# The first up product of an MLP from operands without the norm's factor, and half of a branch product's rows, in a form with seven products

## The chip, the cores and the metric

One NeuronCore of one Trainium2 chip runs the whole program. The metric is device time in microseconds. A time of a kernel is the median of several executions; one further execution is taken by the hardware profiler, and all views of the profile come from that one. TensorE is called PE, VectorE DVE, ScalarE ACT, GpSimd POOL and SyncE SP, as in the profile.

## What is computed

One decoder layer for 512 prompt tokens and 8 x 4 sample tokens, all in float32. Cut to what the change touches:

```python
    # y_a: retention branch, 2048 wide; y_b: gMLP branch, 1024 wide
    merged = sigmoid(zga) * (y_a @ w_br_a) + sigmoid(zgb) * (y_b @ w_br_b)
    h = h + merged @ w_o
    n2 = rmsnorm(h, g_mlp)
    h = h + square(relu(n2 @ w_up)) @ w_down        # w_up: 1024 x 4096, w_down: 4096 x 1024
```

`rmsnorm` multiplies each token by `rsqrt(mean(h*h) + eps)` and each feature by `g_mlp`. The factor of a token is positive, so `relu` may be taken before or after it.

## The kernel before

**Layout.** All activations are kept transposed: a tile holds 128 features on the partitions and all T = 544 tokens in its columns. A product runs over tokens in two halves of TH = 272 columns, so one output tile of 128 features takes two PSUM banks (`Product`, line 303). D = 1024 makes KD = 8 tiles. The MLP's 4096 middle features are worked in four parts f = 0 to 3 of 1024 each: an up product, then a down product that is added to the residual tiles `hs`.

**Precision.** Each float32 operand is split in a high part, rounded to the `float32r` format by ACT, and a low part, the rest, which DVE subtracts (`split`, lines 130 and 131). Each product is then three matmuls: high x high, high x low, low x high.

**The plain form.** `tile_of` (line 327) takes one weight slab (128 x 1024: eight k tiles of one output tile) and issues 8 x 3 x 2 = 48 matmuls of 128 x 272 through `dense` (line 310). `first_two` (line 469) works the first two tiles of a product side by side over the first six k tiles and only then over the last two, so that the last operands of the product may come late. `tiles_from` (line 477) yields all eight tiles.

**The form with seven products.** `fast_run` (line 393) makes two output tiles at once over eight k tiles. Weights, operands and result are looked at as 2 x 2 blocks: the two output tiles by the two halves of the k tiles, those by the two halves of the tokens. Sums and differences of blocks let seven block products stand for eight. A block product is 4 k tiles x 3 matmuls. The operand blocks are B00, B10, B11 and the sums T1 to T4, which `operand_steps` (line 339) makes from a pair of operand tiles k and k + 4: four additions of 272 columns (lines 346 to 355), and the splits of the blocks and of the sums. An operand whose split parts exist already can be handed in as `plain`. The weight blocks of a pair of slabs need a sum that a DMA makes (POOL's queue adds the second slab to two loaded halves, line 207), two additions of 512 columns on DVE (lines 254 and 255) and splits of three slabs and a half, where two plain slabs need two. The block products are drained one by one: copies by ACT (lines 429, 443), and sums on DVE (lines 437 to 459). With two tiles as its target a run adds to these, with a function it returns new tiles with the function applied. A run that is listed in `late` takes three of the four k steps of its first three block products (T1, B10 and B00) before it needs the fourth pair of operands.

**Staging.** Around the change the order of the program is: the sigmoids of the gates (`sig_a`, `sig_b`); the second branch's product (8 plain tiles, line 1188) times `sig_b`; the first branch's product (lines 1193 to 1202: 8 tiles of 16 k tiles each, two weight slabs a tile, all in one PSUM accumulation), times `sig_a`, plus the other branch, split: `merged`; w_o (line 1208), added to the input x, which SP loads again: `hs`. Of each `hs` tile the up operand is made by `scaled_split` (line 525: ACT rounds x times `g_mlp`, DVE makes the rest), without the token's factor, and its square is summed (`add_square`). The first up product (line 1252) is plain. After its first tile `norm2` (line 1219) sums the squares over the features with four small matmuls (line 518) and makes the factor `r2` (root, then reciprocal, line 522). Each up tile is multiplied by it, squared and split (`up`, line 1223): `mid`. `normed_operands` (line 1239) makes, from `hs` and now with the factor in it, the operand sets for the later up products f = 1 to 3, which all run in the form with seven products; two sets are made in the up stage, two in the first down product (line 1258), which is plain. Then come the other parts (line 1298).

The first branch's operands `ya` are 16 tiles of 128 features, stored in DRAM by the heads; `head_tile` (line 1179) loads and splits them while the second branch's product runs, at half-steps given in `HEADS`.

**What sets the order.** `chores` and `later` hang a piece of work on a coming half-step: `tick` runs at every second k tile of `dense` and at every block product of `fast_run`, and calls what is due. `Feed` plans the weights in the order of their use, loads them ahead on SP's queue (five slab buffers, sums looked for two jobs ahead) and splits up to six parts ahead. The program so written is then put in order by a planner, which places each engine's instructions by when it reckons their inputs to be ready, earlier ones in the program first; so neighbouring products can be interleaved on PE. `pin` keeps an instruction behind all that stand before it in the program on its engine. Temporary tiles come from 70 numbered slots (`Slots`, line 65), reused oldest first.

Of the kernel before, what the change touches and what calls it, by code (L numbers as in the profile page):

```python
# [9 lines left out]
F32R = mybir.dt.float32r  # L10
# [4 lines left out]
P = 128  # L15
# [13 lines left out]
GROUPS = 8  # L29
SLAB = 1024  # L30
# [25 lines left out]
HEADS = (0, 2, 4, 6, 8, 10, 12, 14, 16, 18, 20, 21, 22, 23, 24, 25)  # L56
# [37 lines left out]
def layer(tc, a, o):  # L94
    nc = tc.nc
    act, dve, pool, pe = nc.scalar, nc.vector, nc.gpsimd, nc.tensor
    with ExitStack() as ctx:
# [379 lines left out]
        def tiles_from(xs):  # L477

            yield from first_two(xs, (range(KD - 2), range(KD - 2, KD)))
            for _ in range(2, KD):  # L480
                yield tile_of(xs)
# [64 lines left out]
        for m in range(KD):  # L546
            for i in range(2):
                feed.plan("plain", a["w_br_a"][8 * i + m])
        for k in range(8):
            feed.plan("plain", a["w_o"][k])  # L550
        for n in ("w_up", "w_down"):
            for k in range(8):
                feed.plan("plain", a[n][k])
# [8 lines left out]

        plan_up(1, range(4))
# [613 lines left out]
        ya = [None] * 4 * H  # L1177
# [8 lines left out]

        chores([(n, head_tile, k) for k, n in enumerate(HEADS)])
# [4 lines left out]
        merged = []  # L1192
        for m in range(KD):
            ps, t = Product(), get()
            for i in range(2):
                w = feed.take()
                xw = [(*at(w, k * P), *ya[8 * i + k]) for k in range(KD)]
                dense(ps, xw, first=i == 0, last=i == 1)
            dve.tensor_tensor(out=halves(t), in0=ps.all, in1=halves(sig_a[m]), op=ALU.mult)
            dve.tensor_tensor(out=t, in0=t, in1=sig_b[m], op=ALU.add)  # L1200
            put(sig_a[m], sig_b[m])
            merged.append(operand(t))
        for x in ya:
            put(*x)

        hs, hg = [None] * KD, [None] * KD
        total = get()
        for m, ps in enumerate(tiles_from(merged)):
            x = hs[m] = get()
            nc.sync.dma_start(x, a["xT"][m * P : (m + 1) * P, :])  # L1210
            dve.tensor_tensor(out=halves(x), in0=halves(x), in1=ps.all, op=ALU.add)
            hg[m] = scaled_split(x, g(G_MLP, m))
            add_square(total, x, m == 0)
        for x in merged:
            put(*x)
# [7 lines left out]
        def up(ps, k):  # L1223
            t = get()
            if k < 2:
                act.activation(halves(t), ps.all, AF.Relu)
                if k == 0:
                    norm2()
                dve.tensor_tensor(out=t, in0=t, in1=r2s["r"], op=ALU.mult)
            else:  # L1230
                dve.scalar_tensor_tensor(
                    out=halves(t), in0=ps.all, scalar=0.0, in1=halves(r2s["r"]), op0=ALU.max, op1=ALU.mult
                )
            act.activation(t, t, AF.Square)
            return operand(t)

        normed = []

        def normed_operands(k):
            x2 = get(), get()  # L1240
            for i in range(2):
                m = k + 4 * i
                dve.scalar_tensor_tensor(
                    out=x2[i], in0=hs[m], scalar=g(G_MLP, m), in1=r2s["r"], op0=ALU.mult, op1=ALU.mult
                )
# [5 lines left out]
        mid = []  # L1251
        for k, ps in enumerate(tiles_from(hg)):
            mid.append(up(ps, k))
            if k in (3, 5):
                normed_operands(k // 2 - 1)
        for x in hg:
            put(*x)
        for m, ps in enumerate(tiles_from(mid)):
            if m < 2:
                normed_operands(m + 2)  # L1260
            dve.tensor_tensor(out=halves(hs[m]), in0=halves(hs[m]), in1=ps.all, op=ALU.add)
# [293 lines left out]
```

## Time and profile before

| | |
|---|---|
| median of 3 runs | 1239.39 us (1238.52 to 1240.31) |
| the profiled execution | 1238.44 us, of which 1236.8 us are the span of the profile |
| granted TensorE clock | 0.996 |
| second branch's product, first branch's, w_o | about 615.7 to 663.9, to 760.4, to 808.7 us |
| first up product, first down product | to 857.5, to 906.0 us |
| second up product (seven products) | to 948 us |

The profile is of one execution; times in it are microseconds from the start of the span. "L131" is line 131 of the kernel. A group `out<-in` names the program's tiles: `s` a slot, `hl` a split weight slab, `raw` a loaded one, `f` a pair of PSUM banks, `fa` a single bank of `fast_run`. PEld is the weight load that each matmul has, beside the matmuls. A busy time or a mean of one instruction counts each instruction from its start to its end; where instructions of an engine overlap, the distance from start to start is shorter.

### The profile page before, as it was taken

To read this page: it belongs to the slowest core of one execution; us is meant where nothing else is said; L and a number is where in the kernel's file an instruction comes from. 1 tells how busy PE (TensorE), PEld (TensorE's weight loads), DVE (VectorE), ACT (ScalarE), POOL (GpSimd) and SP (SyncE) were. 2 spreads that over 40 slices of the span, in tenths; PEclk is the share of its full clock that TensorE was granted. 3 is DMA by queue.
4 is the path that set the end of the run, shared out by engine and by line. 5 is a ranking of instruction groups with operands and counts; after the bars stand their busy time and mean duration, and the time that the engine had idled before them with its cause. 6 is when DMAs were issued, how large, how long until landed. Compare 5 with 4: busy or idle time off the path is not lost.

```text
span 1236.8 us, 23016 instructions
## 1 busy us (share of the span) xinstructions
PE 1220.6 (99%) x9336; PEld 1192.5 (96%) x9336; DVE 895.9 (72%) x1333; ACT 636.6 (51%) x1082; POOL 92.4 (7%) x127
## 2 busy tenths in 40 slices
PE   9999999999999999999999999999999999999996
PEld 9998998998999999999999999999999999999996
DVE  6986888786697669878663333559459888878956
ACT  6563465365356366655641222455248567476733
POOL 0101101101111112100000000000000000000000
PEclk9999999999999999999999999999999999999998
DMA  8348546636735576665642333324446666764402
GB/s 282 129 156 268 188 136 240 208 131 208 240 115 178 162 220 177 182 160 162 217 156 88 115 107 105 103 69 120 103 111 173 186 180 154 193 183 127 139 1 73
DMA packets 73241, 193.15 MB, mean 156 GB/s; under 512 B 8400, under 2 KB 11728, under 8 KB 73136
## 3 DMA queue, kind: packets, MB, share of 16 engines
q1 hardware_dynamic: 59760, 143.65, 35.1%
q0 software_dynamic: 13376, 48.04, 16.3%
q8 instruction: 73, 1.20, 0.4%
q14 instruction: 32, 0.26, 0.1%
HBM read 165.97 MB, written 25.69 MB: 155 GB/s over the span
## 4 chain that ended last, share of the span: by engine, by line
PE 92%; DVE 4%; ACT 2%; DMA 1%; issue 1%; SPq 0%; DVEq 0%; ACTq 0%
PE f L318 41%; PE fa L407 20%; PE f L407 15%; PE o L494 2%; PE pg L318 2%; PE st L494 2%; PE sc L494 1%; PE su L892 1%; PE so L889 1%; PE so L890 1%; DVE s L522 1%; DVE hl L131 1%; ACT hl L130 1%; PE sp L1124 1%; PE vt L835 1%
## 5 line engine op out<-in xcount | busy, mean ns | idle before, releaser
L318 PE MATMUL f<-s,hl 128*128 128x272 f32 x4320 | 567.2, 289 | 1.2 <-ACT s L528 1.0
L318 PEld LDWEIGHTS f<-s,hl 128*128 128x128 f32 x4320 | 555.1, 188 | 8.2 <-ACT s L528 1.2
L130 ACT CAST hl<-raw 128x1024 fp32r<-128x1024 f32 (+2 forms) x275 | 262.1, 961 | 265.8 <-PE f L318 147.6
L131 DVE TENSOR_TENSOR hl<-raw,hl 128x1024 fp32r<-128x1024 f32 (+2 forms) x275 | 303.3, 1111 | 109.3 <-ACT hl L130 108.9
L407 PE MATMUL fa<-s,hl 128*128 128x272 f32 x2112 | 291.7, 289 | 1.1 <-ACT s L429 0.5
L407 PEld LDWEIGHTS fa<-s,hl 128*128 128x128 f32 x2112 | 274.0, 188 | 2.6 <-ACT s L429 0.7
L407 PE MATMUL f<-s,hl 128*128 128x272 f32 x1584 | 225.0, 289 | 0.7 <-DVE hl L131 0.5
L407 PEld LDWEIGHTS f<-s,hl 128*128 128x128 f32 x1584 | 208.3, 188 | 1.8 <-DVE hl L131 0.8
L130 ACT CAST s<-s 128x544 fp32r<-128x544 f32 (+3 forms) x170 | 97.9, 596 | 28.0 <-DMA s<-ya 6.5
L131 DVE TENSOR_TENSOR s<-s,s 128x544 fp32r<-128x544 f32 (+3 forms) x170 | 107.2, 657 | 4.2 <-ACT s L130 2.8
L893 DVE SCALAR_TENSOR_TENSOR state<-state,su 128x512 f32<-128x512 f32 x64 | 42.9, 681 | 27.3 <-PE su L892 27.2
L130 ACT CAST s<-state 128x512 fp32r<-128x512 f32 x64 | 37.9, 619 | 24.0 <-DMA state<-in_state 8.9
L131 DVE TENSOR_TENSOR s<-state,s 128x512 fp32r<-128x512 f32 x64 | 42.4, 684 | 7.7 <-ACT s L130 4.4
L522 DVE RECIPROCAL s<-s 128x544 f32<-128x544 f32 (+1 forms) x9 | 28.6, 3173 | 18.4 <-ACT s L520 18.4
L207 POOL DMA_DIRECT2D raw<-in_w_up x12 | 10.2, 850 | 412.9 <-DVE s L131 300.0
L454 DVE TENSOR_TENSOR s<-s,f 128x544 f32<-128x544 f32 x44 | 31.4, 713 | 9.4 <-PE f L407 9.1
L644 ACT COPY s<-f 128x544 f32<-128x544 f32 x24 | 14.7, 611 | 38.7 <-PE f L318 38.7
L443 ACT COPY s<-fa 128x272 f32<-128x272 f32 x44 | 16.9, 385 | 32.7 <-PE fa L407 32.5
L255 DVE TENSOR_TENSOR raw<-raw 128x512 f32<-128x512 f32 x44 | 30.4, 694 | 0.6
L254 DVE TENSOR_TENSOR raw<-raw 128x512 f32<-128x512 f32 x44 | 30.5, 695 | 0.4
L318 PE MATMUL pg<-s,s 128*128 128x272 f32 x240 | 30.8, 289 | 0.0
L318 PEld LDWEIGHTS pg<-s,s 128*128 128x128 f32 x240 | 30.3, 188 | 0.1
(175 smaller groups left out, 1103.8 us busy)
## 6 DMA issues: line engine op xcount, KB each, us to landing
raw<-in_w_in SPq DMA_DIRECT2D x58, 512.0 KB, 3.7
state<-in_state SPq DMA_DIRECT2D x32, 512.0 KB, 4.6
out_state_s<-state POOLq DMA_DIRECT2D x32, 512.0 KB, 4.1
raw<-in_w_in SPq DMA_DIRECT2D x60, 256.0 KB, 4.3
raw<-in_w_in POOLq DMA_DIRECT2D x20, 512.0 KB, 5.8
raw<-in_w_up SPq DMA_DIRECT2D x20, 512.0 KB, 3.8
raw<-in_w_down SPq DMA_DIRECT2D x20, 512.0 KB, 4.2
raw<-in_w_up SPq DMA_DIRECT2D x36, 256.0 KB, 3.3
```

What stands on the lines that cost most here:

```text
L130: act.copy(hi, src)
L131: dve.tensor_tensor(out=lo, in0=src, in1=hi.bitcast(F32), op=ALU.subtract)
L254: dve.tensor_tensor(out=t[:, 512:], in0=t[:, 512:], in1=v[:, :512], op=ALU.add)
L255: dve.tensor_tensor(out=t[:, :512], in0=t[:, 512:], in1=v[:, 512:], op=ALU.add)
L318: pe.matmul(ps.p[s], w, x[:, s * TH : (s + 1) * TH], start=first and i == 0 and j == 0, stop=last and i == n - 1 and j == 2, skip_group_ch ...
L407: pe.matmul(ps, a_, b_, start=first and k == j == 0, stop=k == 3 and j == 2, skip_group_check=True)
L443: act.copy(t0[:, hi_half], pa)
L454: dve.tensor_tensor(out=halves(x0), in0=halves(x0), in1=out.all, op=ALU.add)
L494: pe.matmul(ps[:rows, c], u, v, start=i == 0 and j == 0, stop=i == n - 1 and j == 2)
L522: dve.reciprocal(r[:, c], r[:, c])
L644: act.copy(halves(t), ps.all)
L893: dve.scalar_tensor_tensor(out=raw[:, i], in0=raw[:, i], scalar=gamma**LS, in1=ps, op0=ALU.mult, op1=ALU.add)
```

## The change

The first branch's product is cut in its k tiles. The first eight (heads 0 and 1) stay plain: `tiles_from(ya)`, each result copied to a slot by ACT (`sums`). The second eight (heads 2 and 3) go through `fast_run` and are added to these. `head_pair` loads their tiles in pairs and makes the operand sets in steps. The merge with the gates is then done by two DVE operations and a split from the slots, as chores of the next group.

The first up product goes through `fast_run` too, with operands that have `g_mlp` but not the token's factor in them. So w_o's tiles are made in the order 0, 4, 1, 5, 2, 6, 3, 7 (`PAIRED`); of each, ACT makes the scaled tile, which is split, and after the second of a pair the sums are made and split. The factor is applied after `relu`. The operand sets with the factor are now all made in the first down product, which takes its k tiles and its output tiles in the paired order. The first up product's weights are planned as four pairs, the first branch's second half as four pairs.

```diff
+PAIRED = (0, 4, 1, 5, 2, 6, 3, 7)
-HEADS = (0, 2, 4, 6, 8, 10, 12, 14, 16, 18, 20, 21, 22, 23, 24, 25)
+HEADS = (2, 4, 6, 8, 10, 12, 14, 16)
+PAIRS = (2, 8, 14, 20)
+UP = (0, 1)
+NORMED = (5, 10, 18, 25)
...
         for m in range(KD):
-            for i in range(2):
-                feed.plan("plain", a["w_br_a"][8 * i + m])
-        for k in range(8):
+            feed.plan("plain", a["w_br_a"][m])
+        for m in range(8, 16, 2):
+            feed.plan("fast", a["w_br_a"][m], a["w_br_a"][m + 1])
+        for k in PAIRED:
             feed.plan("plain", a["w_o"][k])
...
+        plan_up(0, range(4))
+        for k in PAIRED:
+            feed.plan("plain", a["w_down"][k])
...
+        def head_pair(k):
+            t2 = get(), get()
+            for i in range(2):
+                nc.sync.dma_start(t2[i], ya_d[KD + k + 4 * i])
+            res, held, steps = operand_steps(*t2)
+            y_ops.append((res, held))
+            steps[2:3] = [lambda fn=steps[2]: (fn(), put(*t2))]
+            for n, fn in enumerate(steps):
+                later(3 + n, fn)
...
-        merged = []
-        for m in range(KD):
-            ps, t = Product(), get()
-            for i in range(2):
-                w = feed.take()
-                xw = [(*at(w, k * P), *ya[8 * i + k]) for k in range(KD)]
-                dense(ps, xw, first=i == 0, last=i == 1)
-            dve.tensor_tensor(out=halves(t), in0=ps.all, in1=halves(sig_a[m]), op=ALU.mult)
+        chores([(n, head_pair, k) for k, n in enumerate(PAIRS)])
+        sums = []
+        for ps in tiles_from(ya):
+            sums.append(get())
+            act.copy(halves(sums[-1]), ps.all)
+        for x in ya:
+            put(*x)
+        merged = [None] * KD
+
+        def merge(m, t):
+            dve.tensor_tensor(out=t, in0=t, in1=sig_a[m], op=ALU.mult)
             dve.tensor_tensor(out=t, in0=t, in1=sig_b[m], op=ALU.add)
             put(sig_a[m], sig_b[m])
-            merged.append(operand(t))
+            merged[m] = operand(t)
+
+        for i, t2 in enumerate(fast_run([(y_ops, (sums[2 * i], sums[2 * i + 1])) for i in range(4)], (0,))):
+            if i < 3:
+                chores([(j, merge, 2 * i + j, t) for j, t in enumerate(t2)])
+            else:
+                for j, t in enumerate(t2):
+                    merge(2 * i + j, t)
...
-        for m, ps in enumerate(tiles_from(merged)):
+        for m, ps in zip(PAIRED, tiles_from(merged)):
             x = hs[m] = get()
             nc.sync.dma_start(x, a["xT"][m * P : (m + 1) * P, :])
             dve.tensor_tensor(out=halves(x), in0=halves(x), in1=ps.all, op=ALU.add)
-            hg[m] = scaled_split(x, g(G_MLP, m))
+            t = scaled[m] = get()
+            act.activation(t, x, AF.Copy, scale=g(G_MLP, m))
+            hg[m] = get(F32R), get(F32R)
+            split(*hg[m], t)
             add_square(total, x, m == 0)
+            if m >= 4:
+                x2 = scaled[m - 4], t
+                hg_ops.append(operands(*x2, (hg[m - 4], hg[m])))
+                put(*x2)
...
-                dve.scalar_tensor_tensor(
+                pin(dve.scalar_tensor_tensor(
                     out=x2[i], in0=hs[m], scalar=g(G_MLP, m), in1=r2s["r"], op0=ALU.mult, op1=ALU.mult
-                )
+                ))
...
-        mid = []
-        for k, ps in enumerate(tiles_from(hg)):
-            mid.append(up(ps, k))
-            if k in (3, 5):
-                normed_operands(k // 2 - 1)
+        mid = [None] * KD
+
+        def up(m, t):
+            dve.tensor_tensor(out=t, in0=t, in1=r2s["r"], op=ALU.mult)
+            act.activation(t, t, AF.Square)
+            mid[m] = operand(t)
+
+        for k, t2 in enumerate(fast_run([(hg_ops, AF.Relu)] * 4, (0,))):
+            if k == 0:
+                norm2()
+            for i, t in enumerate(t2):
+                later(UP[i], lambda m=k + 4 * i, t=t: up(m, t))
+        chores([(n, normed_operands, k) for k, n in enumerate(NORMED)])
...
-        for m, ps in enumerate(tiles_from(mid)):
-            if m < 2:
-                normed_operands(m + 2)
+        for m, ps in zip(PAIRED, tiles_from(mid, PAIRED[:6], PAIRED[6:])):
             dve.tensor_tensor(out=halves(hs[m]), in0=halves(hs[m]), in1=ps.all, op=ALU.add)
```

More of the change, by code (lines that the diff above doesn't have):

```diff
@@ L475, in first_two, with tiles_from @@
             return ps
-        def tiles_from(xs):
-            yield from first_two(xs, (range(KD - 2), range(KD - 2, KD)))
+        def tiles_from(xs, *turns):
+            yield from first_two(xs, turns or (range(KD - 2), range(KD - 2, KD)))
             for _ in range(2, KD):
@@ L546, in layer @@
         for m in range(KD):
-            for i in range(2):
-                feed.plan("plain", a["w_br_a"][8 * i + m])
-        for k in range(8):
+            feed.plan("plain", a["w_br_a"][m])
+        for m in range(8, 16, 2):
+            feed.plan("fast", a["w_br_a"][m], a["w_br_a"][m + 1])
+        for k in PAIRED:
             feed.plan("plain", a["w_o"][k])
-        for n in ("w_up", "w_down"):
-            for k in range(8):
-                feed.plan("plain", a[n][k])
         def plan_up(f, ks):
@@ L1176, in layer @@
             put(*held)
-        ya = [None] * 4 * H
+        ya, y_ops = [None] * KD, []
         def head_tile(k):
@@ L1191, in layer @@
             put(*x)
-        merged = []
-        for m in range(KD):
-            ps, t = Product(), get()
-            for i in range(2):
-                w = feed.take()
-                xw = [(*at(w, k * P), *ya[8 * i + k]) for k in range(KD)]
-                dense(ps, xw, first=i == 0, last=i == 1)
-            dve.tensor_tensor(out=halves(t), in0=ps.all, in1=halves(sig_a[m]), op=ALU.mult)
+        chores([(n, head_pair, k) for k, n in enumerate(PAIRS)])
[8 more added lines that the diff above has]
+            dve.tensor_tensor(out=t, in0=t, in1=sig_a[m], op=ALU.mult)
             dve.tensor_tensor(out=t, in0=t, in1=sig_b[m], op=ALU.add)
             put(sig_a[m], sig_b[m])
-            merged.append(operand(t))
-        for x in ya:
-            put(*x)
-        hs, hg = [None] * KD, [None] * KD
+            merged[m] = operand(t)
[5 more added lines that the diff above has]
+                    merge(2 * i + j, t)
+        for _, held in y_ops:
+            put(*held)
+        hs, hg, scaled, hg_ops = [None] * KD, [None] * KD, [None] * KD, []
         total = get()
-        for m, ps in enumerate(tiles_from(merged)):
+        for m, ps in zip(PAIRED, tiles_from(merged)):
             x = hs[m] = get()
@@ L1221, in norm2 @@
             put(total)
[L1223 to L1230, printed above, removed]
-                dve.scalar_tensor_tensor(
-                    out=halves(t), in0=ps.all, scalar=0.0, in1=halves(r2s["r"]), op0=ALU.max, op1=ALU.mult
-                )
-            act.activation(t, t, AF.Square)
-            return operand(t)
         normed = []
@@ L1242, in normed_operands @@
                 m = k + 4 * i
-                dve.scalar_tensor_tensor(
+                pin(dve.scalar_tensor_tensor(
                     out=x2[i], in0=hs[m], scalar=g(G_MLP, m), in1=r2s["r"], op0=ALU.mult, op1=ALU.mult
-                )
+                ))
             normed.append(operands(*x2))
@@ L1249, in normed_operands @@
                 put(r2s["r"])
-        mid = []
-        for k, ps in enumerate(tiles_from(hg)):
-            mid.append(up(ps, k))
-            if k in (3, 5):
-                normed_operands(k // 2 - 1)
+        mid = [None] * KD
[9 more added lines that the diff above has]
+        chores([(n, normed_operands, k) for k, n in enumerate(NORMED)])
         for x in hg:
             put(*x)
-        for m, ps in enumerate(tiles_from(mid)):
-            if m < 2:
-                normed_operands(m + 2)
+        for _, held in hg_ops:
+            put(*held)
+        for m, ps in zip(PAIRED, tiles_from(mid, PAIRED[:6], PAIRED[6:])):
             dve.tensor_tensor(out=halves(hs[m]), in0=halves(hs[m]), in1=ps.all, op=ALU.add)
```

## The prediction

> **What bounds the kernel now.** I read the page first: the engines' shares, then the chain that ended last.
>
> ```profile
> span 1236.8 us, 23016 instructions
> ...
> PE 1220.6 (99%) x9336; PEld 1192.5 (96%) x9336; DVE 895.9 (72%) x1333; ACT 636.6 (51%) x1082; POOL 92.4 (7%) x127
> ...
> PE 92%; DVE 4%; ACT 2%; DMA 1%; issue 1%; SPq 0%; DVEq 0%; ACTq 0%
> ```
>
> PE carries 92% of the chain and is busy for 99% of the span. That is an average, so I then took busy times in the stages that the change touches. I found their limits by counting 48 matmuls a plain tile back and forth from the norm's four small matmuls, which are easy to find. The columns are window, length, PE, PEld, DVE, ACT, POOL, granted clock, DMA share, GB/s.
>
> ```profile
> 663.90:712.00 48.10, 48.10 (x385) 48.10 (x384) 16.51 (x18) 10.35 (x11) 0.00 (x0) 1.00 0.31 100
> 712.00:760.40 48.40, 48.40 (x388) 48.40 (x386) 17.78 (x20) 10.98 (x12) 0.00 (x0) 1.00 0.35 117
> 760.40:808.70 48.30, 48.30 (x387) 48.30 (x386) 25.35 (x31) 17.32 (x23) 0.00 (x0) 1.00 0.30 94
> 808.70:857.50 48.80, 48.80 (x388) 48.64 (x388) 38.42 (x55) 26.58 (x40) 0.84 (x1) 1.00 0.30 86
> 857.50:906.00 48.50, 48.50 (x389) 48.50 (x387) 23.16 (x31) 12.37 (x15) 2.55 (x3) 1.00 0.45 110
> 906.00:948.00 42.00, 42.00 (x337) 42.00 (x336) 33.96 (x53) 31.26 (x54) 2.58 (x3) 1.00 0.56 147
> 948.00:958.50 10.50, 10.50 (x86) 10.50 (x85) 10.32 (x18) 8.52 (x17) 0.87 (x1) 1.00 0.60 145
> ```
>
> The rows are the first branch's product (two), w_o, the first up product, the first down product, the second up product (already in the form with seven products), and one more group of that form. PE's busy time equals the window in every one, at clock 1.00: nothing can be won here but by fewer matmuls, and every microsecond that PE waits afterwards is lost. DVE has much spare time in the first rows (16.5 of 48.1) and none in the last (10.32 of 10.50), and yet PE loses nothing there.
>
> What a matmul costs shows in PE's timeline, from start to start:
>
> ```profile
> 821.52 84.64 PE L318 MATMUL f<-s,hl 128*128 128x272 f32 x672
> 906.00 1.67 PE L407 MATMUL fa<-s,hl 128*128 128x272 f32 x12
> 907.51 1.66 PE L407 MATMUL f<-s,hl 128*128 128x272 f32 x12
> 909.00 3.17 PE L407 MATMUL fa<-s,hl 128*128 128x272 f32 x24
> ```
>
> The plain form: 84.48 us for 672, so 125.7 ns. The other form: 3.00 us for 24, so 125.0 ns. One price serves both, and I take 125.6 ns. The two stages meet at 906.00 without a gap, a plain stage followed by one of seven products, which is what the change makes twice more. The mean durations on the page (289 ns) overlap and are no price.
>
> **What is removed.** Two output tiles over eight k tiles take 2 x 8 x 3 x 2 = 96 matmuls in the plain form, and 7 x 4 x 3 = 84 in the other. The up product has four such pairs and half of the first branch's rows four: 8 x 12 = 96 matmuls, 96 x 125.6 ns = **12.06 us**. The Trainium skill, "TensorE: Matmul & The Clock Gate", section "Back-to-back issue gap", gives N/2.4 + 2.5 ns for an isolated warm matmul, 115.8 ns at 272 columns, by which the gain would be an estimated 11.1 us; the trace's 125.6 differs and decides.
>
> **What is added, and whether it hides.** All of it lies on DVE, ACT and the DMA queues. I price DVE from a stretch in which it runs without a break, again from start to start:
>
> ```profile
> 989.11 0.43 DVE L450 TENSOR_TENSOR s<-s,fa 128x272 f32<-128x272 f32 x1
> 989.47 1.23 DVE L131 TENSOR_TENSOR hl<-raw,hl 128x1024 fp32r<-128x1024 f32 x1
> 990.62 0.71 DVE L454 TENSOR_TENSOR s<-s,f 128x544 f32<-128x544 f32 x1
> 991.25 1.22 DVE L131 TENSOR_TENSOR hl<-raw,hl 128x1024 fp32r<-128x1024 f32 x1
> 992.38 0.44 DVE L131 TENSOR_TENSOR s<-s,s 128x272 fp32r<-128x272 f32 x1
> 992.73 0.43 DVE L437 TENSOR_TENSOR s<-s,f 128x272 f32<-128x272 f32 x1
> 993.08 0.69 DVE L254 TENSOR_TENSOR raw<-raw 128x512 f32<-128x512 f32 x1
> 993.68 0.43 DVE L459 TENSOR_TENSOR s<-s,fa 128x272 f32<-128x272 f32 x1
> 994.06 0.69 DVE L131 TENSOR_TENSOR hl<-raw,hl 128x512 fp32r<-128x512 f32 x1
> 994.67 0.69 DVE L255 TENSOR_TENSOR raw<-raw 128x512 f32<-128x512 f32 x1
> 995.27 0.72 DVE L131 TENSOR_TENSOR s<-s,s 128x544 fp32r<-128x544 f32 x1
> 995.90 0.72 DVE L445 TENSOR_TENSOR s<-s,s 128x544 f32<-128x544 f32 x1
> ```
>
> So 1.14 us for 1024 columns, 0.63 for 544, 0.60 for 512, 0.35 for 272. The weights of a pair cost 3 x 1.14 + 3 x 0.60 = 5.2 us of DVE where two plain slabs cost 2.3; a group of seven products gives PE 84 x 0.1256 = 10.55 us of work.
>
> First branch, second half. Per group: weights 5.2, the sums taken out of PSUM 3 x 0.35 + 2 x 0.63 = 2.3, and two merges of three 544-column operations each, 3.8. The first group has no merge yet (7.5); the next two need 11.3; the last splits plain w_o slabs instead (4.6 + 2.3 + 3.8 = 10.7). DVE falls behind by 0.75 + 0.75 + 0.15 = 1.7 us. After PE's last product there remain these 1.7, one PSUM sum 0.35, two merges 3.8 and the hand-offs to ACT and back, about 1: 6.9 us. w_o's first two tiles run six of eight k tiles first, 72 matmuls = 9.0 us, before they need the last merged tile. So it hides with 2 us to spare, and I take 0.3; if that cover is gone because a group's merges slip behind whole, it is 6.9 + 3.8 - 9.0 = 1.7. Below nothing is excluded: PE waits for nothing there today. The first half's evacuations (0.65 on ACT for each tile) and the operands from the stored heads (four times 4 x 0.35 + 0.35 + 3 x 0.63 = 3.6 us on DVE) fall into a stage with 30 us free: 0, with 0.2 for the entry, at most 1. The heads' loads move from one per tile of the second branch's product to pairs in the stage after it; on SP's queue they stand among weight loads with a 0.31 DMA share: 0.
>
> w_o into up. Here the cover shrinks. Before, the last w_o tile's operand was hidden by 9.0 us of matmuls. Now up's first group runs three of four k steps of its first three products and one more: 27 + 3 = 30 matmuls, 3.77 us, and then wants a sum of the last tile. How such an end of a w_o tile runs, on DVE and on ACT:
>
> ```profile
> 808.98 0.72 DVE L1211 TENSOR_TENSOR s<-s,f 128x544 f32<-128x544 f32 x1 [2.35 <-PE f L318]
> 810.11 1.23 DVE L131 TENSOR_TENSOR hl<-raw,hl 128x1024 fp32r<-128x1024 f32 x1 [0.41 <-ACT hl L130]
> 811.25 0.78 DVE L529 SCALAR_TENSOR_TENSOR s<-s,gcols,s 128x544 fp32r<-128x544 f32 x1
> 811.95 0.72 DVE L504 TENSOR_TENSOR s<-s,s 128x544 f32<-128x544 f32 x1
> ```
>
> ```profile
> 809.03 1.05 ACT L130 CAST hl<-raw 128x1024 fp32r<-128x1024 f32 x1 [3.79 <-issue]
> 809.98 0.75 ACT L528 ACTIVATE s<-s,gcols 128x544 fp32r<-128x544 f32 x1
> 810.63 0.64 ACT L503 ACTIVATE s<-s 128x544 f32<-128x544 f32 x1
> ```
>
> PE ends at about 808.9. A weight slab's cast goes first on ACT (its buffer came free), so the scaled tile, now an ACT step of its own, is there at 0.1 + 0.95 + 0.65 = 1.7 us, its rounded part at 2.35, the square at 3.0. DVE meanwhile: slab 2.2, rest of the tile 2.95, square's sum 3.6, first two sums 4.3; ACT rounds them by 4.95; DVE does the next two sums to 5.0 and the rest of the first two to 5.6. So 5.6 us against 3.77. PE's queue can hold other ready work there: three k steps of the fourth product (9), the last step of another (3), the next group's first product (12), 24 matmuls or 3.0 us, and the planner does put such work forward (the 24 `fa` matmuls at 909.00 are two products of one bank name side by side, out of program order). This is the one wait that the change adds: PE's fourth k step of the second product waits for DVE, and behind it in the queue stands all of up that was not put forward. The cost is between 0 and 1.9, up to 3.0 if a second cast slips in; I take 1.0.
>
> Up into down. The norm's factor is applied after the seven products: per group weights 5.2, sums 0.35 + 0.63, factor and rest for two tiles 4 x 0.63, in all 8.7 of 10.55. The reciprocal was there before. The four operand sets for the next up products leave this stage for the down stage (each 2 x 0.69 + 4 x 0.35 + 0.35 + 3 x 0.63 = 5.0 us, on a DVE that is at 23.16 of 48.50 with two of them in it). They are now pinned to program order on DVE, so they can't be drawn ahead of the last pair's factor; behind them wait only the down product's sums, whose readers come a product later: 0. The last pair's chain of about 5.4 us (relu, factor, square, split, twice overlapped) has 9.0 us of matmuls as cover: 0, at most 1. The last operand set is called 7 of 32 half-steps before the end, 10 us ahead, and needs 5: 0, and 5 if that cover were gone.
>
> The sum: -12.06 + 0.2 + 0.3 + 1.0 = **-10.6**. The profiled execution took 1238.44 us (span 1236.8 and 1.64 around it), which makes 1227.9; the median of the three runs, 1239.39, stands 0.95 above that execution, so the forecast for a median is **1228.8**.
>
> **The rivals.** (1) *DVE sets the pace of the new stages and the covers fail.* 1.7 at w_o, 3.0 at up, 1 at the entry, 1 at down: 6.7 of the 12.06 is given back, 1239.39 - 5.4 = 1234.0. For it: the merges make 11.3 us of DVE in 10.55. Against: the 948.00 window, and three windows in a row within the up stage, of which these are the first and the last, cost PE nothing with DVE full.
>
> ```profile
> 827.00:837.50 10.50, 10.50 (x86) 10.50 (x85) 10.47 (x16) 7.22 (x12) 0.00 (x0) 1.00 0.17 54
> ...
> 848.00:858.50 10.50, 10.50 (x86) 10.50 (x85) 10.50 (x18) 5.35 (x9) 0.84 (x1) 1.00 0.64 137
> ```
>
> There, though, much of DVE's work was not yet wanted by anyone (operand sets for the next product), as the merges are wanted only at w_o.
>
> (2) *The weight sums come late, and the kernel gets slower.* Each pair needs two half loads, then an accumulating DMA on POOL's queue:
>
> ```profile
> L207 POOL DMA_DIRECT2D raw<-in_w_up x12: 842/848/855, 851.3 to 1078.1; - x12
> ...
> DMA to landing us min/median/max: 5.2/5.6/8.6
> ...
> raw<-in_w_up SPq DMA_DIRECT2D x36, 256.0 KB, 3.3
> ```
>
> That is 3.3 + 0.85 + 5.6 = 9.7 us one after the other, within a group's 10.55; at the longest landing 12.7, over by 2.2. If each of the eight new groups paid 2.2, the gain becomes 17.6 - 12.06 = 5.5 us of loss, 1244.9; the point of decision is 12.06 / 8 = 1.5 us a group. SP's queue is where it would show first, a load waiting for a buffer ahead of others. Against: windows 906 and 948 have the same traffic and lose nothing, and the loader in the code looks two jobs ahead for sums to load. The Trainium skill, "SBUF — State Buffer", section "SBUF: two separate sides", says that descriptors for DMAs from GpSimd cannot be written while some DVE operations hold the shared port, so a busier DVE would delay just these transfers. By that rule this rival is the likelier the fuller DVE is; the trace's issue times of 842 to 855 ns, in stretches with DVE nearly full, do not bear it out.
>
> (3) *Nothing measurable*: the same lateness near 1.5 us a group.
>
> **How the numbers follow.** Forecast 0.77, first rival 0.15, third 0.04, second 0.04. About 0.2% (2.5 us) is what a measurement of this kernel can tell from no change. Faster: 0.77 + 0.15 = 0.92; same 0.04; slower 0.04. The low end is the whole 12.06 less 0.9 for the scatter of the runs (1238.52 to 1240.31), 1226.4; the high end takes in the first rival and a microsecond of scatter, 1235.0.
>
> **What would show it.** Right: 96 matmuls fewer, still some 125.6 ns apart; PE busy 12 us shorter; DVE busier by some 60 us (weights 8 x 2.9, the operand sums and PSUM sums the rest); no PE gap over 0.5 us but one of about 1 us where up begins, released by the subtraction of line 131 or its cast. Wrong: PE waiting inside the first branch's second half for a PSUM sum, which is rival (1), or for a weight part whose DMA came last, which is (2). If the up stage begins without any gap, the 1.0 was too much and the time is near 1227.5.

## The result and the profile after

| | before | after |
|---|---|---|
| median | 1238.95 us (1238.33 to 1240.31, 4 runs) | 1225.81 us (1225.55 to 1226.52, 4 runs) |
| profiled execution, its span | 1238.44, 1236.8 us | 1226.52, 1224.8 us |

The ratio is 0.9893, with a 95% interval of 0.9876 to 0.991: the change saves 13.1 us. The direction is as predicted. The gain is larger than predicted, by 3.0 us against the forecast, and the time lies 0.6 us below the low end of the range.

The page of the kernel after, the rows that answer to those of before: engines, then the chain that ended last.

```profile
span 1224.8 us, 23092 instructions
...
PE 1208.8 (99%) x9240; PEld 1181.0 (96%) x9240; DVE 952.1 (78%) x1441; ACT 677.4 (55%) x1160; POOL 99.6 (8%) x135
...
PE 89%; DVE 5%; ACT 3%; DMA 1%; issue 1%; SPq 0%; DVEq 0%; ACTq 0%
```

PE has 9336 - 9240 = 96 matmuls less and is busy 11.8 us less; DVE is busy 56.2 us more, ACT 40.8. PE is as full as before. The stages of the change, by windows (length, PE, PEld, DVE, ACT, POOL, granted clock, DMA share, GB/s): the first branch's plain half; its run of seven products; w_o; the first up product; the first down product.

```profile
663.90:712.60 48.70, 48.70 (x389) 48.70 (x389) 17.87 (x24) 15.95 (x22) 2.55 (x3) 1.00 0.42 110
712.60:757.00 44.40, 44.40 (x357) 44.40 (x356) 38.82 (x56) 20.86 (x30) 0.85 (x1) 1.00 0.43 138
757.00:803.00 46.00, 46.00 (x369) 46.00 (x368) 38.34 (x60) 25.55 (x38) 1.73 (x2) 1.00 0.56 158
803.00:847.00 44.00, 44.00 (x348) 43.63 (x347) 38.80 (x51) 34.06 (x57) 1.71 (x2) 1.00 0.47 136
847.00:894.60 47.60, 47.60 (x382) 47.60 (x381) 39.64 (x64) 20.57 (x32) 2.56 (x3) 1.00 0.51 130
```

In each, PE's busy time equals the window. The view of PE's waits has no entry at all between 600 and 900 us. DVE is at 38 to 40 us in four of the five, where it stood at 17.8, 25.4, 38.4 and 23.2 of about 48 before.

Inside the first branch's run, one row a group:

```profile
712.60:723.20 10.60, 10.60 (x87) 10.60 (x86) 5.45 (x7) 4.18 (x7) 0.00 (x0) 1.00 0.27 100
723.20:733.70 10.50, 10.50 (x86) 10.50 (x85) 10.31 (x18) 5.20 (x8) 0.00 (x0) 1.00 0.32 96
733.70:744.30 10.60, 10.60 (x87) 10.60 (x86) 10.56 (x16) 4.43 (x7) 0.00 (x0) 1.00 0.33 108
744.30:754.80 10.50, 10.50 (x86) 10.50 (x85) 10.30 (x16) 5.65 (x9) 0.85 (x1) 1.00 0.68 223
754.80:765.40 10.60, 10.60 (x87) 10.60 (x86) 8.51 (x13) 3.71 (x5) 0.00 (x0) 1.00 1.00 296
```

DVE is full in the second to the fourth, and PE loses nothing. PE's timeline tells how the end of the run is covered (L411 is the run of seven products, L322 is w_o):

```profile
749.34 2.67 PE L322 MATMUL f<-s,hl 128*128 128x272 f32 x20
...
754.35 1.92 PE L322 MATMUL f<-s,hl 128*128 128x272 f32 x14
756.11 1.67 PE L411 MATMUL fa<-s,hl 128*128 128x272 f32 x12
757.62 4.54 PE L322 MATMUL f<-s,hl 128*128 128x272 f32 x35
762.00 1.65 PE L411 MATMUL fa<-s,hl 128*128 128x272 f32 x12
```

69 matmuls of w_o run before the run's last product does. So PE does not meet DVE's tail at the end of the run; it has spread w_o over it.

The place where a gap of about 1 us was forecast, PE at the end of w_o and the beginning of up:

```profile
803.10 1.30 PE L411 MATMUL fa<-s,hl 128*128 128x272 f32 x9
804.24 2.41 PE L411 MATMUL f<-s,hl 128*128 128x272 f32 x18
806.49 2.04 PE L411 MATMUL fa<-s,hl 128*128 128x272 f32 x15
808.36 0.29 PE L411 MATMUL f<-s,hl 128*128 128x272 f32 x1
808.49 1.42 PE L411 MATMUL fa<-s,hl 128*128 128x272 f32 x10
809.75 1.08 PE L522 MATMUL norm<-s,ones 128*128 128x272 f32 x4
810.46 0.74 PE L411 MATMUL f<-s,hl 128*128 128x272 f32 x3
```

And DVE in the same time:

```profile
803.30 0.72 DVE L1236 TENSOR_TENSOR s<-s,f 128x544 f32<-128x544 f32 x1 [0.15 <-PE f L322]
804.38 1.23 DVE L135 TENSOR_TENSOR hl<-raw,hl 128x1024 fp32r<-128x1024 f32 x1 [0.36 <-ACT hl L134]
805.52 0.44 DVE L351 SCALAR_TENSOR_TENSOR s<-s,s 128x272 f32<-128x272 f32 x1
...
807.82 1.36 DVE L135 TENSOR_TENSOR s<-s,s 128x544 fp32r<-128x544 f32 x2
```

DVE begins with the last w_o tile, splits a weight slab, makes the sums and has their low parts at 809.2, 6.1 us after PE's turn to up. PE asks for them at 810.46. From 803.10 to there it starts 57 matmuls without a gap: 53 of them in 6.65 us, 125.5 ns each, and the norm's four.

### The profile page after: what moved, and what is told of

Same layout as the page of the kernel before. It is cut to its first block, busy times and chain, and to the rows that moved or that the text cites. A ratio compares the mean times of both kernels' runs of the same rounds, so it can differ in the third digit from the quotient of the medians.

```text
span 1224.8 us, 23092 instructions
## 1 busy us (share of the span) xinstructions
PE 1208.8 (99%) x9240; PEld 1181.0 (96%) x9240; DVE 952.1 (78%) x1441; ACT 677.4 (55%) x1160; POOL 99.6 (8%) x135
## 4 chain that ended last, share of the span: by engine, by line
PE 89%; DVE 5%; ACT 3%; DMA 1%; issue 1%; SPq 0%; DVEq 0%; ACTq 0%
PE f L322 33%; PE fa L411 24%; PE f L411 18%; PE o L498 3%; PE pg L322 2%; PE st L498 2%; PE sc L498 1%; PE su L897 1%; PE so L894 1%; PE so L895 1%; DVE hl L135 1%; DMA s<-in_xT 1%; ACT hl L134 1%; DVE s L526 1%; PE sp L1129 1%
## 5 line engine op out<-in xcount | busy, mean ns | idle before, releaser
L322 PE MATMUL f<-s,hl 128*128 128x272 f32 x3552 | 471.9, 289 | 1.5 <-ACT s L1351 0.5
L322 PEld LDWEIGHTS f<-s,hl 128*128 128x128 f32 x3552 | 459.3, 188 | 8.3 <-ACT s L1351 0.8
L135 DVE TENSOR_TENSOR hl<-raw,hl 128x1024 fp32r<-128x1024 f32 (+2 forms) x291 | 318.8, 1103 | 93.9 <-ACT hl L134 93.3
L134 ACT CAST hl<-raw 128x1024 fp32r<-128x1024 f32 (+2 forms) x291 | 274.8, 954 | 171.5 <-PE fa L411 49.1
L411 PE MATMUL fa<-s,hl 128*128 128x272 f32 x2496 | 344.5, 289 | 1.5 <-ACT hl L134 1.1
L411 PEld LDWEIGHTS fa<-s,hl 128*128 128x128 f32 x2496 | 324.0, 188 | 2.8 <-ACT hl L134 1.8
L411 PE MATMUL f<-s,hl 128*128 128x272 f32 x1872 | 265.1, 289 | 0.0
L411 PEld LDWEIGHTS f<-s,hl 128*128 128x128 f32 x1872 | 246.0, 188 | 0.9 <-ACT s L444 0.2
L134 ACT CAST s<-s 128x544 fp32r<-128x544 f32 (+3 forms) x194 | 112.8, 598 | 41.4 <-DVE s L1261 9.7
L135 DVE TENSOR_TENSOR s<-s,s 128x544 fp32r<-128x544 f32 (+3 forms) x194 | 124.4, 660 | 4.9 <-ACT s L134 3.5
L465 ACT ACTIVATE s<-fa 128x272 f32<-128x272 f32 x36 | 14.3, 396 | 30.4 <-PE fa L411 30.4
L902 POOL DMA_DIRECT2D out_state_s<-state x32 | 23.0, 718 | 95.9 <-DVE state L898 88.9
```

The costliest lines, as they stand in the source:

```text
L134: act.copy(hi, src)
L135: dve.tensor_tensor(out=lo, in0=src, in1=hi.bitcast(F32), op=ALU.subtract)
L322: pe.matmul(ps.p[s], w, x[:, s * TH : (s + 1) * TH], start=first and i == 0 and j == 0, stop=last and i == n - 1 and j == 2, skip_group_ch ...
L411: pe.matmul(ps, a_, b_, start=first and k == j == 0, stop=k == 3 and j == 2, skip_group_check=True)
L902: pool.dma_start(o["state_s"][b, c.h].rearrange("(i p) v -> p i v", i=2), raw)
```

## The experiments

What was open after this: whether all that the change adds is really hidden, or saved time in one place covers lost time in another; how much room is left on DVE; and why the time fell by 13.1 us and more when 96 matmuls are worth 12.06.

### The same kernel again

> The changed kernel once more, to size the gain with more executions. Theory A (the gain is the 96 matmuls at 125.6 ns and nothing else, the rest is scatter of the executions): 12.1 us below the kernel before, within 0.6. Theory B (a microsecond is won somewhere besides): 13.1 below, and no execution of it within 12.3 of the median of before.

Measured: 1225.70 us (1225.21 to 1226.97, 4 runs) against 1239.22 for the kernel before, 0.9892 (0.9879 to 0.9906). The gain here is 13.5 us: the surplus of 1 to 1.5 us stays. It is nearer to theory B, though one execution, 1226.97, lies only 12.25 us under the median of before, just within the 12.3 that B excluded.

### One half of the change at a time

The first branch's half alone, with w_o, up and down as before:

```diff
-        for m, ps in zip(PAIRED, tiles_from(merged)):
+        for m, ps in enumerate(tiles_from(merged)):
...
-            t = scaled[m] = get()
-            act.activation(t, x, AF.Copy, scale=g(G_MLP, m))
-            hg[m] = get(F32R), get(F32R)
-            split(*hg[m], t)
+            hg[m] = scaled_split(x, g(G_MLP, m))
```

(and the up and down products as in the kernel before)

> Only the first branch's second half in the form with seven products, the up product plain as before: 48 matmuls fewer. Theory A: 6.0 us below before, no wait of PE between 660 and 910 us. Theory B: if the microsecond stands in this half, 7.0 below. If DVE's 11.3 us of work per 10.55 us group cost PE anything, less than 5.5.

The up product alone, with the first branch as before:

```diff
-            feed.plan("plain", a["w_br_a"][m])
-        for m in range(8, 16, 2):
-            feed.plan("fast", a["w_br_a"][m], a["w_br_a"][m + 1])
+            for i in range(2):
+                feed.plan("plain", a["w_br_a"][8 * i + m])
```

(and the first branch's product and merge as in the kernel before)

> Only the first up product in the form with seven products, the first branch plain as before: 48 matmuls fewer. Theory A: 6.0 us below before. Theory B: if the microsecond stands in this half (operand sets moved to the down stage), 7.0 below. My forecast's wait of 1.0 us at the start of up would make it 5.0.

Measured: branch alone 1230.71 us, 0.9934 (0.992 to 0.9947), 8.5 us saved; up alone 1231.95 us, 0.9941 (0.9929 to 0.9954), 7.3 us saved. Each removes 48 matmuls, 6.03 us. So each half saves more than its matmuls, by 2.5 and 1.3 us (the branch half's 8.5 fits neither 6.0 nor 7.0), and the halves add up to 15.8 us, more than the whole. Something outside the removed matmuls is saved by either half, and only once. The traces place it. From one matmul ahead of the changed products (PE's 4700th, in the second branch's product) to the first of the second up product, PE takes 266.64 us in the kernel before, 260.24 with the branch half and 261.05 with the up half: 6.4 and 5.6 less. From there to PE's last matmul, where no line differs, it takes 321.34, 319.31 and 319.64: 2.0 and 1.7 less.

### The matmuls put back

In each of the eight new groups the T1 product is computed once more, 12 matmuls, before the real one starts afresh in the same bank: 96 in all.

```diff
+                if again:
+                    for k in range(4):
+                        (wh, wl), (xh, xl) = at(w1, 512 + k % 3 * P), ops[k % 3][0]["T1"]
+                        for j, (a_, b_) in enumerate(((wh, xh), (wh, xl), (wl, xh))):
+                            pe.matmul(pc, a_, b_, start=k == j == 0, stop=k == 3 and j == 2,
+                                      skip_group_check=True)
```

> The changed kernel, with one block product of each of the eight new groups done twice (the first result is overwritten): 96 matmuls put back, all else as changed. Theory A: the whole gain is gone, within 0.6 us of before. Theory B: about 1 us below before, as what is won besides the matmuls stays.

Measured: 1237.09 us, 0.9985 (0.9976 to 0.9993). It is 11.4 us over the kernel after run again, 0.7 short of the matmuls' 12.06, which is within the scatter of its executions (1236.84 to 1238.9), and still 2.1 us under the kernel before, though both have 9336 matmuls. What is left of the gain is therefore no matmul of the changed stages.

The same with the branch half alone, 48 put back there:

```diff
-        for i, t2 in enumerate(fast_run([(y_ops, (sums[2 * i], sums[2 * i + 1])) for i in range(4)], (0,))):
+        for i, t2 in enumerate(fast_run([(y_ops, (sums[2 * i], sums[2 * i + 1])) for i in range(4)], (0,), True)):
```

> Branch_only with the 48 matmuls put back (one block product of each of its four groups done twice): as many matmuls as before, but the later stages in the order of branch_only. Theory C: 1.8 to 2.5 us below before, all of it behind the first down product. Theory A (only the count matters): the time of before, within 0.6.

Measured: 1236.43 us against 1239.07, 0.9979 (0.9971 to 0.9988), 2.6 us faster with the same count. The theory that the count alone decides (A) falls.

### The kernel before, run again

If the kernel before varied from one load of the program to the next (D in the expectations), the surplus could be an accident of the first measurement. So it ran once more, unchanged, as a kernel of its own.

> The kernel before once more, for a second profile of it. Theory C (what is won besides the matmuls stands in stages that the change leaves alone, behind the first down product, where PE waits 2.7 us in the profile of before and 0.9 to 2.2 in the changed ones, because the planner puts those stages in another order): the same waits at the same matmuls, 2.7 us, and a median within 0.5 of 1239.2. Rival D (these waits are scatter of one execution): other waits, of another size.

Measured: 1239.33 us, 0.9999 (0.999 to 1.0008). PE's waits behind the first down product, in the kernel before as profiled first (who waited for whom, us in total, times, the longest):

```profile
PE f L407 <- DVE hl L131: 0.5, 1, 0.5
PE fa L407 <- ACT s L429: 0.5, 1, 0.5
PE fa L407 <- ACT s L130: 0.2, 1, 0.2
PE f L407 <- ACT s L1325: 0.2, 1, 0.2
PE f L318 <- ACT s L1325: 0.2, 1, 0.2
```

The same five are in the profile of the second run, at the same matmuls, with the last at 0.5. So they belong to the program, and D falls. PE's waits of the kernel after in those stages:

```profile
PE fa L411 <- ACT hl L134: 0.8, 1, 0.8
PE f L322 <- ACT s L1351: 0.5, 1, 0.5
PE fa L411 <- ACT s L447: 0.3, 1, 0.3
```

Both halves, and the branch half with matmuls put back, have a single wait of 0.7 us. Such a wait costs more than its idle time: from start to start, less the usual 126 ns, the waits behind the first down product make 2.7 us in the kernel before, 2.2 in the kernel after (1.7 when run again), and 0.9 in each of the half kernels. These stages have no line changed.

### The slab buffers' turn

What differs there is the order of PE's matmuls, 2516 of them from the second up product on. `Feed` hands out five buffers for split slabs in turn (`hl_turn`). A pair in the form with seven products takes three full-width buffers where two plain slabs take two, so each four pairs shift the turn by four, that is by four of five. At the later stages the turn stands at 3 in the kernel before, at 2 in either half, at 1 in the kernel after. In the traces both halves, and the branch half with matmuls put back, have one order of these matmuls; the kernel after, run again and with its matmuls put back, has another; the kernel before has a third. Theory (E): the planner puts these stages in another order when the buffers come in another turn, and their waits go with it. The test changes nothing but the turn, one line ahead of the second branch's product:

```diff
+        feed.hl_turn.rotate(-4)
         chores([(n, head_tile, k) for k, n in enumerate(HEADS)])
```

in the kernel before, which brings its turn from 3 to 2.

> The kernel before with one line more: ahead of the second branch's product the turn of the five split-slab buffers is moved on by four. No work is added or left out. The changed kernel's pairs take three full slab buffers instead of two, which moves this turn as well: branch_only and up_only by four, the change by eight, that is by three of five. Theory E (the turn decides in which order the planner puts the later stages, and so their waits): the later stages in the order of branch_only, their waits down from 2.7 to 0.9 us, and the time 1.8 to 2.7 us below before, 1236.4 to 1237.3. If the turn has nothing to do with it: the time of before within 0.6.

Measured: 1236.25 us (11 runs) against 1238.90 (21 runs), 0.998 (0.9971 to 0.9989): 2.65 us for a line that moves no work, and 0.15 below the time expected at the least. The trace puts it in the later stages: from PE's first matmul to the second up product it takes 904.83 us, as before (904.84), and from there to the last 319.12 instead of 321.34, 2.2 us less. (The other 0.4 of the medians is not located.) The later matmuls come in the order of the half kernels, and PE has their one wait:

```profile
PE f L318 <- ACT s L1326: 0.7, 1, 0.7
```

The kernel after with the line as follows, from turn 1 to turn 2:

```diff
+        feed.hl_turn.rotate(-1)
         chores([(n, head_tile, k) for k, n in enumerate(HEADS)])
```

> The changed kernel with the turn moved on by one more, to where branch_only has it. Theory E: the later stages wait 0.9 us instead of 1.7 to 2.2, the time 0.8 to 1.3 below the changed kernel, 1224.4 to 1225.0: faster than both kernels. If the order of the later stages is not set by the turn: 1225.7 within 0.5.

Measured: 1224.42 us (1224.12 to 1224.8), 0.9885 (0.9872 to 0.9899). It is the fastest of all and beats both kernels: 14.5 us under the kernel before beside it, where the kernel after was 13.1 and 13.5 under. It too has one wait there, 0.7 us. With both at turn 2 the change is worth 1236.25 - 1224.42 = **11.8 us**, and between PE's first and last matmul 1223.95 - 1211.79 = 12.16. Of this, 0.31 lies ahead of the 4700th matmul, and so of the changed products; from there to the second up product it is 11.83, and in the later stages, now in one order, 0.02. So the changed stages give the 96 matmuls, 12.06, less 0.2.

The kernel after brought to turn 4:

```diff
+        feed.hl_turn.rotate(-3)
         chores([(n, head_tile, k) for k, n in enumerate(HEADS)])
```

> The changed kernel with the turn moved on by three, a place that none of the kernels so far has had. Theory E: waits in the later stages of another size than 0.9, 1.7 to 2.2 or 2.7, at other matmuls, within 1.5 us of the changed kernel in either direction; up to the first down product no difference over 0.3.

Measured: 1227.86 us (1226.25 to 1228.56), 0.9911 (0.9898 to 0.9925), 2.1 us slower than the kernel after, where at most 1.5 was expected. Up to the second up product its trace takes 893.64 us, 0.2 more than the kernel after (893.44); the later stages take 322.65, 3.55 more than at turn 2 (319.10). Its two waits of 1.4 and 0.9 us, 2.65 from start to start where turn 2 has 0.86, explain 1.8 of that. The rest is what they do to the clock, told in the last section.

### What hides the chain at the start of up

The matmuls of up's first two groups and of the norm are kept in program order on PE; no work is changed.

```diff
-                        pe.matmul(ps, a_, b_, start=first and k == j == 0, stop=k == 3 and j == 2,
-                                  skip_group_check=True)
+                        ins = pe.matmul(ps, a_, b_, start=first and k == j == 0, stop=k == 3 and j == 2,
+                                        skip_group_check=True)
+                        if held_order and turn[0] < 2:
+                            pin(ins)
```

(`turn[0]` counts the groups of the run; the norm's matmuls are pinned likewise)

> The changed kernel with the matmuls of up's first two groups and of the norm held in the order of the program, so that nothing can be put forward into the wait for the last w_o tile's sums. If putting forward is what hid the chain: PE waits 6.0 - 3.8 = 2.2 us behind the first 30 matmuls of up, and another 0.3 to 0.6 for a bank's copy between two products of one bank, 2.2 to 3.0 in this stage. Rival (the chain was shorter than I reckoned): no wait over 0.5 there.

Measured: 1229.12 us, 0.9918 (0.9905 to 0.9932), 3.4 us over the kernel after; its profiled execution, 1227.78 us, is 2.2 over that of the kernel after run again (1225.59). From the 4700th matmul to the second up product the two traces differ by 2.8 us (257.51 against 254.70). PE's timeline:

```profile
806.01 0.54 PE L413 MATMUL fa<-s,hl 128*128 128x272 f32 x3
806.38 0.29 PE L413 MATMUL f<-s,hl 128*128 128x272 f32 x1
808.75 0.89 PE L413 MATMUL f<-s,hl 128*128 128x272 f32 x5 [2.09 <-DVE s L135]
809.48 1.68 PE L413 MATMUL fa<-s,hl 128*128 128x272 f32 x12
811.64 0.64 PE L413 MATMUL fa<-s,hl 128*128 128x272 f32 x3 [0.47 <-ACT s L452]
```

Without the matmuls put forward PE runs 31 and then stands for 2.24 us longer than a matmul takes (808.75 - 806.38 - 0.13), and once more for 0.6: 2.9 us. The chain is there, of the length that was reckoned, and what hides it in the kernel after is that 26 matmuls (57 - 31) are ready and put forward: 22 of the run's and the norm's four.

### How much room DVE has

Each merge makes three further multiplications of 544 columns into a tile that nobody reads: 24 of them, 24 x 0.63 = 15.1 us of DVE.

```diff
         def merge(m, t):
+            junk = get()
+            for _ in range(3):
+                dve.tensor_tensor(out=junk, in0=t, in1=sig_a[m], op=ALU.mult)
+            put(junk)
             dve.tensor_tensor(out=t, in0=t, in1=sig_a[m], op=ALU.mult)
```

> The changed kernel with three more 544-column multiplications on DVE in each of the eight merges, into a tile that nobody reads: 24 x 0.63 = 15.1 us more of DVE in the first branch's second half, where a group already has 11.3 us of DVE work for 10.55 of PE. By my account 2.2 us were to spare at its end and some 3 in the first group: PE loses about 10 us. Rival (the merges have more room, since w_o's matmuls of the first six k tiles are put forward and its tiles need little of DVE): under 5 us.

Measured: 1235.19 us, 0.9969 (0.9957 to 0.9981), 9.5 us over the kernel after. By windows:

```profile
744.30:754.80 10.50, 8.76 (x67) 8.26 (x66) 10.50 (x17) 4.95 (x7) 0.00 (x0) 1.00 0.49 148
754.80:765.40 10.60, 7.76 (x58) 7.10 (x56) 10.60 (x16) 2.96 (x4) 0.85 (x1) 1.00 0.95 268
765.40:776.00 10.60, 8.93 (x67) 8.53 (x68) 10.60 (x19) 1.99 (x4) 0.00 (x0) 1.00 0.52 196
```

Now DVE fills every window and PE does not. Of 15.1 us some 5.6 are hidden and 9.5 are paid, as expected (about 10). So the engine that the first rival named is the next to bound this stage, 5 to 6 us away.

### One step further

The first down product is put in the form with seven products too: 48 matmuls less. In this form the operand sets of the later up products read the residual tiles after the down product's sums, in part, and not before them, so that the later parts compute something else and their operands wait for those sums.

```diff
-        for m, ps in zip(PAIRED, tiles_from(mid, PAIRED[:6], PAIRED[6:])):
-            dve.tensor_tensor(out=halves(hs[m]), in0=halves(hs[m]), in1=ps.all, op=ALU.add)
+        for _ in fast_run([(mid0, (hs[2 * i], hs[2 * i + 1])) for i in range(4)], (0,)):
+            pass
```

> The changed kernel with the first down product in the form with seven products too: 48 matmuls fewer again, 6.0 us of PE. By my account DVE is then the bound: up needs 4 x 11.1 + 3.5 and down 4 x 12.5, 98 us of DVE in 84 of PE, and the next up product waits for the last operand set: 8 us or more lost, so 2 us slower than the changed kernel, 1227 to 1230. Rival (the later stages take up the backlog): 1219.7.

Measured: 1240.64 us (1239.26 to 1242.92), 1.0016 (1.0007 to 1.0025), 15 us slower than the kernel after. The expectation missed. PE was busy 38.2 of 45 us in the window from 845 on and 38.9 of 45 in the next, with DVE at 40 in both. How much of this is DVE's work and how much the added order between sums and operand sets is not told apart, and part of it is a fall of the granted clock, told in the last section. So as a size it says nothing. That this plain product was a cover for DVE's work fits the full DVE, but is not shown by this run.

## Why the prediction was right, and where it failed

The main term and the direction came out as predicted; the sum did not, and two steps of it failed: the price of 1.0 us for w_o into up, and the assumption, made without a word, that the stages behind the change keep their time.

**Removed: 96 matmuls, 12.06 us.** Right: 9336 to 9240, and 803.10 to 806.49 is 3.39 us for 27, still 125.6 ns each. With the turn held alike the whole change measures 11.8 us, and in the traces the changed stages take 11.8 to 11.9 us less at every turn compared (266.64 before, 254.70 to 254.86 after).

**Added work on DVE and ACT, hidden.** Right: DVE 56.2 us more, some 60 reckoned, with DVE full in the groups where 11.3 us of work in 10.55 was reckoned.

**Entry, 0.2, and first branch into w_o, 0.3.** No wait of PE is seen at either place. The tail was priced for a PE that comes to w_o only after the run's last product. In fact w_o begins 14 us before.

**w_o into up, 1.0.** This step failed. The chain was sized well, 5.6 us against 6.1, but not its cover: the 24 matmuls that the text counts as able to be put forward were taken for half, and PE put forward 26. (Of the 24, 21 were among these 26; the norm's four were not counted.) The gap is 0. With the order held it is 2.24 us, where the text has 1.9 for a cover of 30 matmuls alone, and a second wait of 0.6, which the text does not have. The sign announced for this, a begin of up without any gap, is what the profile shows, and the 1227.5 named with it (by the text's own sum 1228.8 - 1.0 = 1227.8) is nearer to the time than the forecast.

**Stages not touched keep their time.** This was never written down, and it failed as well: it is why even a price of nothing for every wait, 1239.39 - 12.06 = 1227.3, is 1.5 us too high. The later stages were put in another order, because the change takes slab buffers in another number, and lost 0.5 us less to waits in the profiled execution, 1.0 less in the one run again. By medians the turn explains 2.65 us that the kernel before loses against the best turn tried, and 1.0 to 1.3 that the kernel after loses: 1.35 to 1.65 of net gain. Together with the 11.8 this makes the 13.1 to 13.5 measured; as differences of the same medians they must add up so, and it is the traces that place them. The two first profiled executions have 11.93 us less in the changed stages and 0.67 less in the later ones, but 0.53 more ahead of the changed products, and so 12.07 between PE's first and last matmul; both kernels run again have 11.94, 1.51 and 0.25 more, 13.20. The low end of the range, the whole 12.06 and 0.9 of scatter, had no place for it.

**From the profiled execution to the median, +0.95.** This is no constant of a kernel: the kernel after has its profiled execution above its median, 1226.52 against 1225.81. 1.5 us of waits that did not come and 1.35 or more of the turn account for the 3.0 by which the forecast is too high; what is left is of the size of this term's error. It is not told apart from the scatter ahead of the changed products.

**The rivals.** The first, DVE setting the pace, did not happen, but the run with more DVE work shows it 5 to 6 us away. The second, late weight sums, did not happen either. POOL's accumulating issues in the changed stages of the kernel after:

```profile
L211 POOL DMA_DIRECT2D raw<-in_w_up x8: 847/855/873, 753.9 to 885.3; - x8
...
DMA to landing us min/median/max: 5.3/7.1/8.4
```

They and the first branch's four land later than the issues quoted of before (a median of 7.1 us against 5.6), and no matmul waits for them. The Trainium skill, "SBUF — State Buffer", section "SBUF: two separate sides", has the writing of such DMAs' descriptors held up while DVE runs an operation in a mode that uses two ports, so not by every busy DVE. Here the issues took 847 to 873 ns in stages with DVE busy for 38 to 40 us of 44 to 48, where up's in the kernel before took 842 to 855 and down's up to 883, so the trace shows no hold-up; which of DVE's operations here use that mode, no run shows.

## What to carry to other kernels

Price a change by the work that it takes from the engine that is never idle, and then ask of each wait whether the planner has other ready work to put into it: count that work and, where it exceeds the wait, price the wait at nothing. A change that takes shared buffers in another number re-orders stages that it does not touch, here by 1 to 3.4 us between the turns tried: before a small gain is put down to the change, give both kernels the same turn, and then try the other turns, which cost one line each. Why turn 2 is the good one was not found, and turn 0 was not tried.

## What the runs showed of the chip

Two short waits of PE close together can cost more than their length. In the profiled execution of the kernel after at turn 4, PE's timeline in the later stages:

```profile
1109.84 1.66 PE L322 MATMUL f<-s,hl 128*128 128x272 f32 x12
1112.89 0.51 PE L411 MATMUL fa<-s,hl 128*128 128x272 f32 x2 [1.39 <-ACT hl L134]
1114.34 1.18 PE L411 MATMUL fa<-s,hl 128*128 128x272 f32 x7 [0.94 <-DVE hl L135]
1115.32 2.92 PE L322 MATMUL f<-s,hl 128*128 128x272 f32 x12
```

and its windows, the granted clock third from the end:

```profile
1111.00:1115.00 4.00, 1.67 (x12) 1.24 (x11) 3.74 (x6) 4.00 (x7) 0.84 (x1) 1.00 0.76 230
1115.00:1120.00 5.00, 5.00 (x30) 5.00 (x30) 3.17 (x7) 3.32 (x6) 0.86 (x2) 0.66 0.95 174
```

After 4 us in which PE was busy for 1.67, the granted clock fell to 0.66 for the next 5, and twelve matmuls took 2.92 us where twelve took 1.66 just before, though PE had never stood for longer than 1.39 us at a time. In closer windows of the same trace the clock is 1.00 from 1111.90 to 1115.31, with PE busy for 1.48 us, then 0.50 from 1115.31 to 1118.72, and 1.00 again: 3.41 us at half the clock, which by that would cost 1.7 us (an estimate). With the 1.8 us of waits this makes the 3.55 by which these stages are longer than at turn 2. It seems not to happen in every execution: of the four, those with a mean clock of 0.997 took 1226.25 and 1227.82 us, the others 1227.91 at 0.996 and 1228.56 at 0.995, the profiled one. Of the kernel with the first groups in held order, 1227.78 and 1228.33 us stand at 0.997, 1229.12 to 1229.77 at 0.995, but the one that was profiled is at 0.997 and keeps its clock, so that a fall there is not shown. In the last experiment it stands in a stretch with PE half idle:

```profile
900.00:905.00 5.00, 2.10 (x10) 1.66 (x10) 5.00 (x9) 1.71 (x3) 0.00 (x0) 0.94 0.43 111
905.00:910.00 5.00, 3.85 (x18) 3.11 (x16) 5.00 (x11) 2.70 (x4) 0.00 (x0) 0.72 0.22 66
910.00:915.00 5.00, 4.72 (x23) 4.51 (x24) 4.44 (x7) 1.39 (x3) 0.86 (x1) 0.66 0.66 180
```

In closer windows these are two stretches at 0.50, from 904.39 to 907.80 and from 911.21 to 914.63, 3.41 us each, with 1.00 between them; in the 3.41 us ahead of each PE was busy for 1.10 and 2.20 us.

The Trainium skill, "TensorE: Matmul & The Clock Gate", section "What's actually happening", gives a free-running window of about 3.4 us, and its section "Why this matters for your kernels" advises against idle gaps of over some 3 us. The stretches of 3.41 us agree with such a window, but not with a single gap of that length as the condition: 3.41 us in which PE was busy for 1.10 to 2.20 were enough. How little busy time it takes was not measured, and that the window falls differently from one execution to the next is not shown by these runs.
